# One unit of w_down operands made in the first down phase, and one less beside the gate/up phase of pass 1

## Chip, cores and metric

One core of a Trainium2 chip. The metric is the device time of one execution in microseconds (us), median of several runs. The kernel before: 2275.49 us (2274.35 to 2276.27, 3 runs).

## The reference

```python
x: (8, 1024, 1024)   w_gate, w_up: (1024, 4096)   w_down: (4096, 1024)   # float32
gate = x @ w_gate
up = x @ w_up
gate = 0.5 * gate * (1 + np.tanh(np.sqrt(2 / np.pi) * (gate + 0.044715 * gate ** 3)))
h = gate * up
return (h @ w_down).astype(np.float32)
```

## The kernel before

The 8192 tokens go through in eight passes of 1024. Each pass has a gate/up stage and a down stage. Both use fast (Strassen-like) matrix products in 16-bit floats: passes 0 to 2 with one level of splitting (7 products instead of 8), later passes with a scheme that needs 24 products. Its operands are sums of blocks of the weights, which are made once, in passes 1 to 3, beside the matmuls that run anyway, and kept in DRAM. For w_down this work is cut into eight **units**; one unit is 19 sums on VectorE, six signed copies on ScalarE, and 24 stores of 128 KB (`wd_quads`). Its steps are handed out one by one at set places of the instruction streams.

```python
def wd_unit(u, raw, free):               # raw: where its inputs are loaded; free: output buffers
    nb, j = divmod(2 * u, 8)
    blk = raw.rearrange("p (k c j h) -> p k c j h", k=2, c=2, j=2)
    ...
    def load():
        for k, c, v in ((0, 0, 0), (1, 0, 1), (1, 1, 5)):
            nc.sync.dma_start(out=blk[:, k, c], in_=wdop[2 * v + nb][:, j : j + 2, :])
        nc.gpsimd.dma_start(out=blk[:, 0, 1], in_=wd_eo[0][:, 2 * u : 2 * u + 2, HH:])
    ...
    def step(i):
        stores()                         # of what the step before made, from SyncE
        n, op, a, b = WD_SUMS[i]
        v = at[n] = free.popleft()
        combine(node(n), op, node(a), node(b))               # VectorE
        ...                              # every third step also a signed copy on ScalarE
    return load, [lambda i=i: step(i) for i in range(len(WD_SUMS))] + [stores]

UNITS_ONE = {1: ((0, 4, 4), (1, 108, 4)), 2: ((3, 20, 6),)}   # gate/up: (unit, load at, spacing)
UNITS_DOWN = {1: (2,), 2: (4, 5)}                             # down
UNITS_UP = {3: (6, 7)}
```

In gate/up of passes 1 and 2 there are 16 column tiles of 14 products each, so 224 places; a unit is loaded at the named place and its steps begin 20 places later. GpSimd issues the raw loads of w_gate and w_up for the tiles to come (1 MB each, cast from 32 to 16 bits) at the thirteenth product of each odd tile.

A down stage of these passes is seven products in two halves each, so 14 half-products of 4 x 8 matmuls with 512 columns. In the first one (pass 0), half of w_down (`wd_half`) lies on chip; `half_sum` makes further operands of it in place, `half_store` writes them out, and SyncE issues four DMA transposes for the next pass at the fifth half-product:

```python
half_work = {                            # (half-product, group)
    ...
    (3, 1): [lambda: half_sum(3, 0)], (3, 3): [lambda: half_sum(3, 1)],
    (5, 1): [lambda: half_sum(4, 0)], (5, 3): [lambda: half_sum(4, 1)],
    ...
}
if nb == 0 and g == 0 and p + 1 < NPASS:
    ...
    if v == (2 if p < FAST - 1 else 0):
        transpose_x(p + 1)               # SyncE, 4 transposes
```

## Time and profile before

Stage lengths, from the starts of TensorE's groups in its timeline. Read the second column against the third: where the same matmuls take longer, TensorE waits.

| stage | us | the same matmuls at 215.8 ns each | units made in it |
|---|---|---|---|
| down, pass 0 | 96.69 | 96.7 | 0 |
| gate/up, pass 1 | 205.17 | 193.4 | 2 |
| down, pass 1 | 96.69 | 96.7 | 1 |
| gate/up, pass 2 | 195.58 | 193.4 | 1 |
| down, pass 2 | 96.69 | 96.7 | 2 |

### The profile page before, as it was taken

Reading aid. Unit: us, or ns where it says so; the run is one execution under the profiler, and the core shown is the slowest. Engines: PE = TensorE matmul, PEld = TensorE weight load, DVE = VectorE, ACT = ScalarE, POOL = GpSimd, SP = SyncE. Lnnn points to the kernel's source line nnn. Section 1 sums busy time; section 2 is a strip of 40 time slices with the busy share of each in tenths; the row PEclk is TensorE's granted clock in tenths of the full one; section 3 lists DMA queues with packets and bytes.
Section 4 is the critical chain, followed back from the end, with each engine's and each line's share of the span. In section 5 each row is a group of like instructions: output and inputs, shape, how many; then the busy total and the mean of one; then the engine's idle time right before and its main releaser. Section 6 shows DMA issues by size and latency. Waiting matters only on the chain.

```text
span 2272.0 us, 42804 instructions
## 1 busy us (share of the span) xinstructions
PE 2251.1 (99%) x16639; PEld 1625.5 (72%) x16639; DVE 1560.5 (69%) x2188; ACT 956.3 (42%) x1868; POOL 693.0 (31%) x826
## 2 busy tenths in 40 slices
PE   8999999999999999999999999999999999999999
PEld 4444444444444444888888888888888888888888
DVE  5576368785488864777776677766776667866674
ACT  4443136552155531666115551256403653055520
POOL 1343013430033310455105450145402543034520
PEclk9999999999999999999999999999999999999999
DMA  9998969999999999999998989989999889998876
GB/s 231 176 210 203 263 165 242 247 261 300 254 243 234 244 322 341 336 333 382 309 333 281 312 312 304 333 269 325 298 321 323 278 315 311 323 317 275 282 290 227
DMA packets 308796, 643.50 MB, mean 283 GB/s; under 512 B 79152, under 2 KB 185648, under 8 KB 288048
## 3 DMA queue, kind: packets, MB, share of 16 engines
q1 hardware_dynamic: 253536, 567.36, 73.3%
q0 software_dynamic: 55056, 73.41, 19.4%
q8 instruction: 130, 2.13, 0.4%
q14 instruction: 74, 0.61, 0.1%
HBM read 575.67 MB, written 138.41 MB: 314 GB/s over the span
## 4 chain that ended last, share of the span: by engine, by line
PE 90%; DVE 5%; DMA 3%; issue 1%; ACT 1%; SPq 0%; POOL 0%; DVEq 0%; POOLq 0%; ACTq 0%
PE ps L843 40%; PE ps L1091 20%; PE ps L621 16%; PE ps L983 13%; DMA ring<-in_w_up_dram 2%; DVE ring L350 2%; DVE tmp L640 1%; DVE h_s L278 1%; DMA wd_quads<-x_sums 1%; PE ps L1190 1%; DVE h_a L658 1%; DVE x_sums L278 1%; DMA h_a<-in_x_dram 0%; DMA w_ops<-h_s 0%; ACT ps L637 0%
## 5 line engine op out<-in xcount | busy, mean ns | idle before, releaser
L843 PEld LDWEIGHTS <-ring 128*128 128x128 f16 x8320 | 814.1, 98 | 94.4
L820 POOL TENSOR_TENSOR h_a<-tmp 128x256 f16<-128x256 f32 x640 | 468.3, 750 | 840.3 <-ACT tmp L808 832.7
L843 PE MATMUL ps<-x_sums,ring 128*128 128x256 f16 x5760 | 655.8, 273 | 0.0
L805 DVE TENSOR_TENSOR tmp<-tmp,ps 128x512 f32<-128x512 f32 x640 | 414.4, 683 | 149.3 <-PE ps L843 94.4
L621 PEld LDWEIGHTS <-ring 128*128 128x128 f16 x2632 | 257.5, 98 | 326.6 <-issue 18.4
L790 ACT COPY tmp<-ps 128x512 f32<-128x512 f32 x520 | 303.8, 584 | 237.7 <-PE ps L843 164.8
L621 PE MATMUL ps<-x_sums,ring 128*128 128x512 f16 x1504 | 345.0, 380 | 10.9 <-DVE tmp L640 7.0
L808 ACT ACTIVATE tmp<-tmp 128x256 f32<-128x256 f32 x640 | 263.8, 418 | 173.1 <-DVE tmp L803 79.5
L843 PE MATMUL ps<-x_b,ring 128*128 128x256 f16 x2560 | 305.6, 273 | 0.0
L647 POOL TENSOR_TENSOR h_a<-tmp 128x512 f16<-128x512 f32 x94 | 158.5, 1686 | 362.8 <-ACT tmp L645 223.9
L803 DVE TENSOR_TENSOR tmp<-ps,tmp 128x512 f32<-128x512 f32 x240 | 165.4, 689 | 145.5 <-ACT tmp L790 99.7
L621 PE MATMUL ps<-x_b,ring 128*128 128x512 f16 x1128 | 259.3, 379 | 0.1
L1091 PEld LDWEIGHTS <-h_a 128*128 128x128 f16 x2240 | 219.1, 98 | 25.4
L983 PE MATMUL ps<-ring,h_a 128*128 128x512 f16 x1024 | 222.3, 379 | 0.0
L1091 PE MATMUL ps<-ring,h_a 128*128 128x256 f16 x1920 | 216.1, 273 | 0.0
L983 PEld LDWEIGHTS <-h_a 128*128 128x128 f16 x1152 | 112.7, 98 | 135.9
L640 DVE TENSOR_TENSOR tmp<-ps,tmp 128x512 f32<-128x512 f32 x188 | 127.7, 684 | 114.2 <-ACT tmp L632 111.4
L1148 ACT ACTIVATE tmp<-ps 128x512 f32<-128x512 f32 x60 | 35.4, 597 | 362.5 <-PE ps L1091 274.4
L1160 DVE SCALAR_TENSOR_TENSOR tmp<-ps,tmp 128x512 f32<-128x512 f32 x120 | 81.1, 690 | 97.5 <-PE ps L1091 66.7
L632 ACT COPY tmp<-ps 128x512 f32<-128x512 f32 x188 | 109.8, 584 | 85.9 <-PE ps L621 82.5
L350 DVE TENSOR_TENSOR ring<-ring 128x1024 f16<-128x1024 f16 x188 | 134.2, 726 | 13.8 <-DMA ring<-in_w_up_dram 9.6
L1091 PE MATMUL ps<-ring,x_sums 128*128 128x256 f16 x1120 | 126.4, 273 | 0.0
(94 smaller groups left out, 1535.1 us busy)
## 6 DMA issues: line engine op xcount, KB each, us to landing
ring<-w_ops SPq DMA_DIRECT2D x480, 512.0 KB, 5.0
ring<-wd_quads SPq DMA_DIRECT2D x110, 1024.0 KB, 7.1
ring<-wd_ops SPq DMA_DIRECT2D x35, 1024.0 KB, 7.5
out_dram<-tmp SPq DMA_DIRECT2D x128, 256.0 KB, 6.3
w_ops<-h_s SPq DMA_DIRECT2D x128, 256.0 KB, 6.9
ring<-in_w_gate_dram POOLq DMA_DIRECT2D x23, 1024.0 KB, 11.1
ring<-in_w_up_dram POOLq DMA_DIRECT2D x23, 1024.0 KB, 17.9
wd_quads<-x_sums SPq DMA_DIRECT2D x136, 128.0 KB, 6.2
```

The costliest lines, as they stand in the source:

```text
L350: nc.vector.tensor_tensor(o, a, b, op)
L621: nc.tensor.matmul(ps(b, w), lhs[:, k], rhs[:, k, :], start=(first and k == 0), stop=(k == KH - 1), skip_group_check=True,)
L640: nc.vector.tensor_tensor(o, ps("b", w), o, ADD)
L647: nc.gpsimd.tensor_tensor(hq[TO[n]][:, i, :], tmp[:, t[n, 1]], tmp[:, t[n, 0]], MUL)
L790: nc.scalar.copy(tmp[:, t[o[1]]], ps_all[:, bank[o[2]]])
L803: nc.vector.tensor_tensor(d, b, a, SUB)
L805: nc.vector.tensor_tensor(d, a, b, ADD if o[4] == "add" else SUB)
L808: nc.scalar.activation(d, d, GELU, scale=GSC)
L820: nc.gpsimd.tensor_tensor(h, tmp[:, t[o[1]], MQ : 2 * MQ], g, MUL)
L843: nc.tensor.matmul(ps_all[:, bank[c], w * MQ : (w + 1) * MQ], lhs[:, w, k], rhs[:, k], start=(first and w == 0 and k == 0), stop=(k == KH ...
L983: nc.tensor.matmul(ps_all[:, bank[b, g]], lhs[:, j, g * P : (g + 1) * P], dc[:, n, :], start=(first and j == 0), stop=(j == NP - 1), skip_ ...
L1091: nc.tensor.matmul(ps_all[:, bank[c], m * MQ : (m + 1) * MQ], lhs[:, j, m * P : (m + 1) * P], rhs[:, j, :], start=(first and j == 0 and m ...
```

## The change

Intent: take one unit away from the only stage where TensorE waits much, and make another one in the first down stage, where half of w_down is on chip and VectorE has time. The in-place half-sums of that stage must then come later, as they overwrite what the unit reads.

```diff
     def wd_unit(u, raw, free):
-        blk = raw.rearrange("p (k c j h) -> p k c j h", k=2, c=2, j=2)
+        if raw is not None:
+            blk = raw.rearrange("p (k c j h) -> p k c j h", k=2, c=2, j=2)
...
+                if raw is None:
+                    return wd_half[k][:, j : j + 2, c * MQ : (c + 1) * MQ]
...
-    UNITS_ONE = {1: ((0, 4, 4), (1, 108, 4)), 2: ((3, 20, 6),)}
+    UNITS_ONE = {1: ((0, 60, 6),), 2: ((2, 20, 6),)}
...
-    UNITS_DOWN = {1: (2,), 2: (4, 5)}
+    UNITS_DOWN = {0: (4,), 1: (1,), 2: (3, 5)}
...
-            (3, 1): [lambda: half_sum(3, 0)],
-            (3, 3): [lambda: half_sum(3, 1)],
...
-            (5, 1): [lambda: half_sum(4, 0)],
-            (5, 3): [lambda: half_sum(4, 1)],
-            (6, 0): [lambda: half_store(4)],
-            (7, 0): [lambda: half_store(6)],
+            (6, 2): [lambda: half_sum(3, 0)],
+            (7, 0): [lambda: half_sum(3, 1)],
+            (7, 2): [lambda: half_store(4)],
+            (8, 0): [lambda: half_sum(4, 0)],
+            (8, 2): [lambda: half_sum(4, 1)],
+            (9, 0): [lambda: half_store(6)],
...
-            free = deque(xc[:, j * 512 : (j + 1) * 512] for j in range(24, 38))
+            free = deque(xc[:, j * 512 : (j + 1) * 512] for j in range(24 if p else 32, 38))
+            free.append(spare)
             for i, u in enumerate(UNITS_DOWN[p]):
-                load, fs = wd_unit(u, xc[:, i * 8192 : i * 8192 + 4096], free)
-                steps.setdefault(0, []).append(load)
+                load, fs = wd_unit(u, xc[:, i * 8192 : i * 8192 + 4096] if p else None, free)
+                if p:
+                    steps.setdefault(0, []).append(load)
```

## The prediction

> **What bounds the kernel now.** I read the page first (busy shares, slices), then the table of stretches cut at the stage borders, then TensorE's timeline for every idle gap, then the chain of waits just ahead of the largest gap, and last the DMA issues and VectorE's timeline of the stretch that receives the moved work.
>
> ```profile
> span 2272.0 us, 42804 instructions
> PE 2251.1 (99%) x16639; PEld 1625.5 (72%) x16639; DVE 1560.5 (69%) x2188; ACT 956.3 (42%) x1868; POOL 693.0 (31%) x826
> ```
>
> TensorE is idle for 2272.0 - 2251.1 = 21 us in all, and busy TensorE is at its pace: in the first down phase 96 matmuls of 512 columns start at 228.23 us and the next group at 248.95, so 20.72 / 96 = 215.8 ns each. Whatever this change wins must come out of those 21 us and out of matmuls slowed by a lower clock. Where they are, the stretches tell (first down phase, gate/up of pass 1, down of pass 1, gate/up of pass 2; columns: length, busy us and count of TensorE, its weight loads, VectorE, ScalarE, GpSimd, then granted clock, DMA share, GB/s):
>
> ```profile
> 214.42:311.11 96.69, 96.69 (x449) 43.83 (x448) 46.92 (x51) 11.86 (x20) 5.67 (x5) 1.00 0.89 235
> 311.11:516.28 205.17, 197.09 (x897) 87.83 (x896) 161.83 (x260) 117.46 (x196) 71.40 (x45) 0.99 0.94 243
> 516.28:612.98 96.70, 96.70 (x450) 43.83 (x448) 45.00 (x62) 14.76 (x26) 5.96 (x6) 1.00 0.99 273
> 612.98:808.56 195.58, 194.44 (x898) 87.58 (x896) 156.70 (x241) 114.45 (x190) 65.19 (x46) 1.00 1.00 252
> ```
>
> Gate/up of passes 1 and 2 has the same 896 matmuls, at 215.8 ns at best 193.4 us. Pass 2 takes 195.58, pass 1 takes 205.17. Both make as many entries of the later passes' w_gate/w_up operands; the difference is that pass 1 also makes two units of w_down operands and pass 2 one. Both down phases are without a gap (448 x 215.8 ns = 96.7 us). TensorE's timeline gives the gaps (start, length, group, idle before it):
>
> ```profile
> 390.12 4.65 PE L621 MATMUL ps<-x_sums,ring 128*128 128x512 f16 x20 [1.28 <-DVE tmp L640]
> 442.18 6.06 PE L621 MATMUL ps<-x_sums,ring 128*128 128x512 f16 x20 [2.78 <-DVE tmp L640]
> 494.70 4.48 PE L621 MATMUL ps<-x_sums,ring 128*128 128x512 f16 x20 [1.09 <-DVE tmp L640]
> 664.52 4.48 PE L621 MATMUL ps<-x_sums,ring 128*128 128x512 f16 x20 [0.20 <-DVE tmp L640]
> ```
>
> Pass 1 has ten such gaps from 338 to 495 us, 7.9 us together; pass 2 three, 0.9 us. The worst also leaves a slow group: 6.06 us for 20 matmuls that take 4.48 elsewhere. The chain of waits before it:
>
> ```profile
> 413.67 0.88 POOL ring L335
> 414.55 22.91 DMA ring<-in_w_up_dram
> ...
> 438.16 0.42 DVE spare L278
> ```
>
> The raw w_up load was issued at 413.67, just after the second unit's four loads (410.62 to 412.21), and landed only after 22.91 us. VectorE was then late with the weight sums, the unit's own operation on "spare" stood in line among them, and PSUM was emptied late.
>
> **What the Trainium skill says.** "TensorE: Matmul & The Clock Gate", section "Wait — 56ns, not 53.3ns?", gives 215.7 ns from start to start at 512 columns when warm; the trace's 215.8 agrees, so nothing is to be had from busy TensorE. The same page, section "Part 1: The HAM clock gate", says that an idle window of about 3.4 us brings the half clock back; here the granted clock fell to 0.72 in 442 to 448 us after a gap of only 2.78 us, so the measurement decides: a gap of this size costs 1.58 us on top of itself. "VectorE: DVE Perf Modes", section "The perf-mode tier table", gives 1224 ns for a 16-bit tensor_tensor of 2048 elements; the trace has 1.22. "DMA: Bandwidth & Descriptors", section "Queues, rings and completion order", says that all transfers issued from SyncE share one row of rings and are taken in ring order; the trace agrees, SyncE's stores landing in order of issue, and this is what my main doubt rests on.
>
> **The change, part by part.** There are eight units before and after. Unit 4 moves to the first down phase, and the others shift: pass 1 gate/up makes unit 0 alone (one step every 6 products from product 80, as pass 2 does from product 40) instead of 0 and 1; pass 1 down still makes one unit, pass 2 gate/up one, pass 2 down two. No matmul is added or removed.
>
> *Removed from pass 1 gate/up:* 19 VectorE sums at 0.36 us from start to start (VectorE's timeline in pass 1 down: six from 544.37 to 546.51), 6.8 us of VectorE, six ScalarE copies at 0.62 (3.8 us), 24 stores of 128 KB and four loads of 256 KB. VectorE would be 162 - 6.8 = 155 us busy there, as in pass 2 (156.70). The products at which steps fall modulo 14 are the same set as in pass 2. So I take pass 2 as the measured model: 205.17 - 195.58 = **9.6 us saved**, from 8.5 to 10.3 because the phase of the steps against the pairs differs.
>
> *Added to the first down phase:* the same 19 sums and six copies, without loads, as both halves lie on chip. VectorE has 96.7 - 46.9 = 50 us idle, ScalarE 85 us: by busy time it is free. But there are only seven buffers (six of 512 columns and the spare one) instead of fourteen in pass 1, and a step comes every 5/6 of a slot of eight matmuls (1.73 us), that is every 1.44 us. A buffer is free when its store has landed, and SyncE's order has the four transposes in the middle:
>
> ```profile
> 243.25 0.49 SPq L454 DMA_DIRECT2D wd_ops<-x_sums  x1
> 243.80 19.58 SPq L255 DMA_TRANSPOSE x_b<-x_half  x4
> 263.43 0.60 SPq L454 DMA_DIRECT2D wd_ops<-ring  x1
> 264.13 1.53 SPq L454 DMA_DIRECT2D wd_ops<-x_sums  x1
> 265.76 1.39 SPq L530 DMA_DIRECT2D ring<-wd_ops  x1
> ```
>
> I followed the buffers by hand through the code. Steps 0 to 12 run from 232 to about 249 us. Step 13 takes the buffer of the copy made in step 9, whose store is issued behind the transposes. I put the end of the transposes at 263.4 + 3.4 = 266.8 us (estimate: six 128 KB stores at 0.33 us each and one 1 MB store at about 3.7 us, moved later, go ahead of them, less the 2 to 3 us that the DMA engines idled about 235 us). The store is issued at 267.4 and, as after the transposes of pass 1 (2.5 us from issue to landing), lands at 269.9. So VectorE stands for some 20 us, does steps 13 to 17 by 272, step 18 after one more landing at 273, then the two half_sum of 1.14 us by 275.5. TensorE reads them in its tenth half-product, which starts at 214.42 + 9 x 6.907 = 276.58: **1 us to spare**. The next 1 MB load for the eleventh, issued at 265.76 and landed at 277.2 now, comes behind the last unit store, at about 274, with one 1 MB store and some 0.7 MB of small stores queued before it: landing at 282.5 to 283.5 against a need at 283.49. **No slack.** ScalarE's copy of step 15, which waits for the same landings, also holds the PSUM copies of P6 until about 272, needed at 273.1.
>
> *Sum:* 2275.5 - 9.6 + expected stall. I give no stall 60%, about 1.5 us 25%, about 4 us 15%: 1.0 us. That makes 2266.9 us.
>
> **Rivals.** *A: the saving is whole and the down phase swallows the unit.* For it: 50 us of idle VectorE, and that half_sum was moved back on purpose. Time 2275.5 - 9.6 = 2265.9, or 2264.5 if pass 1 loses still less than pass 2. *B: a wait takes the place of the removed one:* seven buffers behind the transposes stop VectorE and SyncE, and TensorE waits in the tenth and eleventh half-product. For it: the two margins of 1 and 0 us; against it: only a transpose end past 268 us makes over 2 us of it. Time 2268 to 2272. *C: pass 1 keeps its gaps,* because the entries and not the second unit cause them. Against it: pass 2 has as many entries with 0.9 us, and pass 1 has no gap before the first unit's steps begin. Time 2271 to 2275.
>
> **Range and chances.** The ceiling of a gain is pass 1's 205.17 - 193.4 = 11.8 us, 0.5%; over 2% is out of reach. The best case is 2275.5 - 11.8 = 2263.7; a stall of 4 us with 8.5 saved gives 2271.0. I take 2263.5 to 2271.5. A loss of 2% would need 45 us of stall, and nothing that I found can hold TensorE so long.
>
> **What would show it.** Right: gate/up of pass 1 at 195 to 197 us with gaps under 2 us in total and no slow group; VectorE's idle time on x_sums for the landing of wd_quads stores rising by some 20 us in the first down phase; transposes issued until 266 to 268; that phase 96.7 us, or up to 4 us longer with gaps at its tenth or eleventh half-product. Wrong: gate/up of pass 1 still above 199, the first down phase above 101 us, or a new gap in pass 2 or later, where I expect no difference.

## The result

The changed kernel took **2267.85 us** (median of 4 runs, 2267.33 to 2269.77) against 2274.92 us of the kernel before in the same rounds (4 runs). The ratio is 0.9972, 95% interval 0.9954 to 0.9989. Ratios here are the mean time of one kernel's fast runs over that of the other's of the same rounds, so not quite the ratio of the medians quoted. All runs that ratios are taken from are fast (none is over 1.5% above the fastest of its kernel). Where the interval of a ratio leaves out 1, the small difference is clear of the runs' noise. The kernel before had medians of 2272.8 to 2273.5 us beside the experiments.

The page of the changed kernel, to be held against the two lines shown of before:

```profile
span 2265.6 us, 42805 instructions
PE 2249.9 (99%) x16639; PEld 1625.8 (72%) x16639; DVE 1560.5 (69%) x2188; ACT 956.5 (42%) x1868; POOL 687.4 (30%) x825
```

TensorE's idle time fell from 21 to 15.7 us. The table of stretches, cut at the same four stage borders:

```profile
213.82:312.46 98.64, 97.03 (x450) 43.76 (x448) 54.10 (x70) 14.89 (x26) 5.67 (x5) 1.00 0.97 262
312.46:510.42 197.96, 194.76 (x897) 87.62 (x896) 155.82 (x241) 114.56 (x190) 64.38 (x44) 1.00 0.89 232
510.42:607.12 96.70, 96.70 (x450) 43.83 (x449) 45.08 (x62) 14.75 (x26) 5.96 (x6) 1.00 1.00 271
607.12:802.42 195.30, 194.28 (x898) 87.56 (x897) 154.56 (x241) 114.62 (x190) 66.46 (x46) 1.00 1.00 254
```

Gate/up of pass 1 became 7.21 us shorter, the first down stage 1.95 us longer. VectorE's busy time moved as the sums demand: 7.2 us more in the first row, 6.0 less in the second. The rest of the 6.4 us between the two spans lies where the change touches nothing: 0.6 before the first gate/up stage, 0.3 in gate/up of pass 2, 0.3 in the last stage. The first of these varied from 30.0 to 31.0 us over all the profiles, so nothing is built on it.

TensorE's timeline of the changed kernel. Two gaps are new, in the first down stage, and of the ten in pass 1's gate/up four are left:

```profile
273.89 3.61 PE L989 MATMUL ps<-ring,h_s 128*128 128x512 f16 x16 [1.20 <-ACT tmp L914]
284.82 20.89 PE L989 MATMUL ps<-ring,h_a 128*128 128x512 f16 x96 [0.41 <-DMA ring<-wd_ops]
...
389.83 4.48 PE L625 MATMUL ps<-x_sums,ring 128*128 128x512 f16 x20 [2.08 <-DVE tmp L644]
427.16 4.48 PE L625 MATMUL ps<-x_sums,ring 128*128 128x512 f16 x20 [0.53 <-ACT ps L641]
```

**The first down stage.** SyncE's timeline, the row of the four transposes and the load for the eleventh half-product (L534):

```profile
249.11 0.32 SPq L454 DMA_DIRECT2D wd_ops<-x_sums  x1
249.74 18.59 SPq L255 DMA_TRANSPOSE x_b<-x_half  x4
268.43 1.01 SPq L486 DMA_DIRECT2D wd_quads<-x_sums  x2
...
278.28 0.39 SPq L534 DMA_DIRECT2D ring<-wd_ops  x1
```

VectorE's, at step 13 of the unit:

```profile
271.90 0.43 DVE L278 TENSOR_TENSOR x_sums<-x_sums 128x512 f16<-128x512 f16 x1 [19.92 <-DMA wd_quads<-x_sums]
```

ScalarE's, at the copy of step 15 (L505) and the two snapshots of P6 (L914) that stand behind it:

```profile
272.72 0.63 ACT L505 ACTIVATE x_sums<-ring 128x512 f16<-128x512 f16 x1 [19.45 <-DMA wd_quads<-x_sums]
273.26 1.07 ACT L914 ACTIVATE tmp<-ps 128x512 f32<-128x512 f32 x2
```

The stores of steps 9 to 12 stood behind the transposes until 268.4 us; both engines waited almost 20 us for buffers; and the snapshots (the copies of product P6 out of PSUM, the memory in which TensorE sums up) came 1.2 us after TensorE wanted their banks. Why SyncE reached the transposes so late: in all fourteen traces no SyncE transfer is issued before the one eight issues earlier has landed, so it never has more than eight under way. Its last five issues from 245.13 to 249.74 us each begin within 0.06 us of such a landing (245.07 to 249.72). Whether the chip or the program sets the limit is not shown.

The wait that sets the stage's length is the last one. Without any wait the eleventh half-product would begin 10 x 6.907 us into the stage, at 282.89 us; its load, issued behind the unit's stores at 278.28, landed at 284.77, 1.88 us late. The 1.20 us before it only hides most of this.

**Gate/up of pass 1.** The chain of waits before the gap of 2.08 us:

```profile
365.29 20.49 DMA x_sums<-in_w_down_dram
385.77 0.02 issue
385.80 0.43 DVE x_sums L278
```

This is the unit's own load, which GpSimd issued just behind two raw loads (362.25 and 363.18 us). It landed only after 20.49 us, and the unit's first sum, already in VectorE's line, held up everything behind it for 1.79 us. In the kernel before it was the other way round: there the raw load came late behind the unit's.

### The profile page after: what moved, and what is told of

It reads as the page before. It is cut to its first block, busy times and chain, and to the rows that moved or that the text cites. A ratio compares the mean times of both kernels' runs of the same rounds, so it can differ in the third digit from the quotient of the medians.

```text
span 2265.6 us, 42805 instructions
## 1 busy us (share of the span) xinstructions
PE 2249.9 (99%) x16639; PEld 1625.8 (72%) x16639; DVE 1560.5 (69%) x2188; ACT 956.5 (42%) x1868; POOL 687.4 (30%) x825
## 4 chain that ended last, share of the span: by engine, by line
PE 91%; DVE 5%; DMA 2%; SPq 1%; issue 1%; ACT 0%; POOL 0%; DVEq 0%; ACTq 0%
PE ps L847 40%; PE ps L1097 20%; PE ps L625 19%; PE ps L989 11%; DVE ring L350 2%; DVE tmp L644 1%; DMA x_sums<-in_w_down_dram 1%; SPq L255 1%; DVE h_s L278 1%; DMA wd_quads<-x_sums 1%; PE ps L1196 1%; DVE h_a L662 1%; DVE x_sums L278 0%; DMA h_a<-in_x_dram 0%; DMA ring<-wd_ops 0%
## 5 line engine op out<-in xcount | busy, mean ns | idle before, releaser
L651 POOL TENSOR_TENSOR h_a<-tmp 128x512 f16<-128x512 f32 x94 | 153.4, 1632 | 375.1 <-ACT tmp L649 254.4
```

Source lines behind the costliest of these rows:

```text
L651: nc.gpsimd.tensor_tensor(hq[TO[n]][:, i, :], tmp[:, t[n, 1]], tmp[:, t[n, 0]], MUL)
```

## The experiments

The theory: the gain is what one unit less is worth in pass 1's gate/up, less a wait in the first down stage that comes from seven buffers whose stores stand behind the transposes. Its rivals: the place of loads, not the number of units, costs pass 1; a unit costs the same wherever it is put; the down stage's wait has another cause. Diffs are against the changed kernel unless the text says otherwise.

### Transposes later

```diff
-                        if v == (2 if p < FAST - 1 else 0):
+                        if v == ((3 if p == 0 else 2) if p < FAST - 1 else 0):
```

> The changed kernel with the four transposes of the first down phase issued at the seventh half-product instead of the fifth, so that the unit's stores no longer stand behind them. My theory (the phase's 1.95 us over its 96.69 come from SyncE's order: stores behind transposes, seven buffers): VectorE's 19.9 us wait at step 13 shrinks to under 6 us, ScalarE's snapshots come on time, the first down phase takes 96.7 to 97.0 us, the rest stays, so about 1.9 us less than the changed kernel (some 2266 us). Rival (the buffers alone are too few, or the DMA engines are simply full there): the phase stays above 98 us.

Measured: 2266.64 us (5 runs), ratio to before 0.997 (0.9957 to 0.9982). The first down stage took 97.74 us. The gap at the ninth half-product was gone, VectorE's longest wait in the unit was 6.11 us (under 6 expected), but another gap had grown:

```profile
284.78 20.89 PE L989 MATMUL ps<-ring,h_a 128*128 128x512 f16 x96 [0.87 <-DMA ring<-wd_ops]
```

That is the eleventh half-product's 1 MB load, now itself behind the transposes: issued at 275.56, landed at 284.73 us. So the order on SyncE is the cause, and half of the cost was put back by the same cause in another place (the last experiment removes this half too); the expected 96.7 to 97.0 was missed by 0.7.

### The unit's load ahead of the raw loads

```diff
-    UNITS_ONE = {1: ((0, 60, 6),), 2: ((2, 20, 6),)}
+    UNITS_ONE = {1: ((0, 46, 6),), 2: ((2, 20, 6),)}
```

> The changed kernel with unit 0 in gate/up of pass 1 begun at product 46 instead of 60 (same place modulo 14, one column tile earlier), so that its GpSimd load is issued ahead of the raw gate/up loads of the fourth tile and not behind them. My theory (the 2.08 us gap at 389.83 comes from that load landing 20.5 us after issue, which VectorE meets 20 products later): the load lands in under 9 us, no gap above 0.6 us in that stage, pass 1's gate/up takes 195.5 to 196.3 us instead of 197.96, about 2 us less in all. Rival (pass 1 has less room on VectorE than pass 2 whatever the load does): it stays at 197.5 or more, with the gap one tile earlier.

Measured: 2265.37 us, ratio 0.9963 (0.995 to 0.9977). The load landed in 8.1 us. Gate/up of pass 1 took 195.73 us, with three gaps left, of which the largest is

```profile
377.29 4.48 PE L625 MATMUL ps<-x_sums,ring 128*128 128x512 f16 x20 [0.67 <-ACT ps L641]
```

So pass 1 with one unit is as good as pass 2, and the 2.08 us were the load's place. The largest gap left was 0.67 us and not under 0.6.

### Both

> Both edits, the late transposes and the early load. If the two costs are independent: 1.9 + 2.0 us less than the changed kernel, some 2264 us, 0.5% under the kernel before; first down phase 96.7 to 97.0, gate/up of pass 1 195.5 to 196.3. If one hides the other: no better than the better of the two alone.

Measured: 2263.36 us, ratio 0.9955 (0.9943 to 0.9968). First down stage 96.69 us, without a gap, gate/up of pass 1 195.62 us. The load for the eleventh half-product landed at 283.69 us this time, 0.1 us before its need at 283.82. The two savings add up, as they should if the costs are independent.

### The addition alone

```diff
-    UNITS_ONE = {1: ((0, 60, 6),), 2: ((2, 20, 6),)}
+    UNITS_ONE = {1: ((0, 4, 4), (1, 108, 4)), 2: ((3, 20, 6),)}
-    UNITS_DOWN = {0: (4,), 1: (1,), 2: (3, 5)}
+    UNITS_DOWN = {0: (4,), 1: (2,), 2: (4, 5)}
```

> The kernel before with the added part alone: unit 4 is made in the first down phase as in the change, and once more where the kernel before makes it; pass 1's gate/up keeps its two units. My theory: first down phase 98 to 99 us as in the changed kernel, gate/up of pass 1 still 205 us, so 2 us slower than the kernel before (ratio 1.001). Rival (part of the gain comes from the moved half-sums and stores of the first down phase and not from the unit removed): gate/up of pass 1 shorter than 204 us.

Measured: 2273.88 us against 2273.53, ratio 1.0004 (0.9992 to 1.0017). The first down stage took 99.32 us, 2.63 more than before and a little over what was expected. But gate/up of pass 1 took 203.73 us, the rival's side of the line, and pass 2's 195.04, which is why the time hardly moved. Two profiles of the kernel before have 205.17 and 204.99. By the line drawn beforehand for the second of them (205.2 again within 0.3 us, below) the addition did shorten pass 1, by some 1.3 us, and five runs that are no slower in spite of 2.63 us more in one stage agree. But this rests on one profile of the stage (the changed kernel's same stage differed by 1.25 us between two), and its cause was not looked for. The next run has the change's gate/up of pass 1 without the added unit, and there the stage is as short as in the change: its 7.2 us don't need the addition.

### The removal, with the unit put into the down stage of pass 1

```diff
-    UNITS_DOWN = {0: (4,), 1: (1,), 2: (3, 5)}
+    UNITS_DOWN = {1: (1, 4), 2: (3, 5)}
```

> The removal without the addition: as the changed kernel, but unit 4 is made as a second unit of pass 1's down phase and not in the first down phase (correct result). My theory: first down phase 96.7 us, gate/up of pass 1 198 us as in the change, down phase of pass 1 96.7 us as pass 2's with two units, so about 1.9 us less than the changed kernel, some 2266 us. Rival (a unit costs wherever it is put, some 2 us a piece): the down phase of pass 1 takes 98 us or more and the time is that of the changed kernel.

Measured: 2273.66 us against 2273.52, ratio 1.0 (0.9987 to 1.0014): the whole gain was gone in the runs. The profiled one was the fastest of them (2270.19 us, mean granted clock 1.000; the other four 2272.58 to 2274.29 us at 0.998 to 0.999), so the profile shows less than the whole loss. The first down stage was back at 96.69 us and gate/up of pass 1 took 197.97 us as in the change, but the down stage of pass 1 took 101.14:

```profile
579.50 1.89 PE L989 MATMUL ps<-ring,h_a 128*128 128x512 f16 x8 [1.95 <-DVE tmp L918]
583.56 26.06 PE L989 MATMUL ps<-ring,h_a 128*128 128x512 f16 x120 [2.17 <-DVE tmp L918]
```

The first half of the theory holds: without the added unit the first down stage has no wait. The expectation for the second place was wrong. VectorE there waited 13.81 us for a store behind that stage's transposes and, with two units on fifteen buffers, four times more for landings; ScalarE's snapshots stood behind the unit's copies, VectorE's additions behind them. I had taken pass 2's down stage, which makes two units without a gap, as the model, and overlooked that its transposes are issued in the first half-product, ahead of all unit stores, while those of pass 1 come in the fifth, as in pass 0.

### The kernel before with unit 1 begun earlier

Against the kernel before; the unit's loads and steps move together by 10 of the 224 places:

```diff
-    UNITS_ONE = {1: ((0, 4, 4), (1, 108, 4)), 2: ((3, 20, 6),)}
+    UNITS_ONE = {1: ((0, 4, 4), (1, 98, 4)), 2: ((3, 20, 6),)}
```

> The kernel before with unit 1 of pass 1's gate/up begun at product 98 instead of 108, its loads some 10 us ahead of the raw loads instead of just before them; still two units in that stage. Rival to the change (what costs pass 1 is where the unit's loads fall among the raw loads, not that there are two units): the raw load lands in 19 us instead of 22.9, the 2.78 us gap at 442 us and the slow group after it (1.58 us) go, pass 1's gate/up falls to 201 us or less. My theory: that one gap goes or shrinks, but the other gaps (some 5 us) stay, because two units load VectorE more thickly; 200.5 to 203 us, 2 to 4.5 us less than the kernel before and still slower than the change with its own load mended.

Measured: 2269.95 us against 2273.52, ratio 0.9985 (0.9973 to 0.9998). Gate/up of pass 1 took 201.58 us. No gap above 1.3 us was left in it; where 2.78 us and the slow group had been, there are

```profile
440.20 4.48 PE L621 MATMUL ps<-x_sums,ring 128*128 128x512 f16 x20 [0.73 <-ACT ps L637]
453.31 4.65 PE L621 MATMUL ps<-x_sums,ring 128*128 128x512 f16 x20 [0.86 <-ACT ps L637]
```

The raw load landed in 21.5 us, not in the expected 19, but that sufficed. So 3.6 of the 9.4 us by which pass 1 exceeded the mended one-unit stage (205.17 against 195.73) went when the second unit's loads were moved, and 5.85 us (201.58 - 195.73) are left for two units at spacing four against one at six. The edit moved the unit's steps too, so that the 3.6 us are the loads' alone is argued from the gap that went and not shown. The rival has a good third of the truth.

### One unit, but as thickly as before

```diff
-    UNITS_ONE = {1: ((0, 60, 6),), 2: ((2, 20, 6),)}
+    UNITS_ONE = {1: ((0, 46, 4),), 2: ((2, 20, 6),)}
```

> The changed kernel with unit 0 loaded at product 46 and its steps every 4 products instead of every 6. It tells whether the smaller gaps of the kernel before (0.2 to 1.3 us, at 338 to 403 us and 469 to 495 us) come from how thickly the steps stand rather than from the number of units. If thickness: gaps of 0.3 to 1.3 us return in the 76 products of the unit, gate/up of pass 1 198 to 200 us. If not: as with the early load alone, 195.5 to 196.3 us.

Measured: 2267.28 us, ratio 0.9972 (0.9958 to 0.9985); gate/up of pass 1 198.31 us, with gaps such as

```profile
402.21 4.48 PE L625 MATMUL ps<-x_sums,ring 128*128 128x512 f16 x20 [0.86 <-ACT ps L641]
427.42 4.65 PE L625 MATMUL ps<-x_sums,ring 128*128 128x512 f16 x20 [0.85 <-ACT ps L641]
```

That is 2.58 us more than the same unit at spacing six. Twice this, 5.2 us, would be most of the 5.85 us left by the run before it, if the costs of two units add, which no run tests. A unit hurts by how thickly its steps stand, and two units, which share the place for their inputs, fit into 224 places only thickly.

### The unit's copies on VectorE

```diff
+                if raw is None:
+                    nc.vector.tensor_scalar(
+                        v.rearrange("p (j h) -> p j h", j=2), node(m), float(sign), None, MUL
+                    )
+                else:
                     nc.scalar.activation(...)
```

> The changed kernel with the unit's six copies in the first down phase made by VectorE instead of ScalarE, so that ScalarE's snapshots of P6 no longer stand behind a copy that waits for a store. It tells whether the phase's 1.95 us is that one hold or whether three margins lie one behind the other. My theory (all three hang on the transposes' end): the gap at the ninth half-product goes, but gaps at the tenth (half-sums done about 277 us against a need at 276) and the eleventh (load landing about 285 against 283) take its place, and the phase stays at 98.3 to 99.0 us. Rival (the hold alone): the phase falls to 97.2 us or less.

Measured: 2269.22 us against 2272.81, ratio 0.9983 (0.9966 to 0.9999). The first down stage took 100.08 us. The gap at the ninth half-product is gone and those at the tenth and eleventh have taken its place, each with the releaser expected:

```profile
277.36 7.34 PE L994 MATMUL ps<-x_sums,h_s 128*128 128x512 f16 x32 [1.17 <-DVE x_sums L451]
286.32 20.89 PE L994 MATMUL ps<-ring,h_a 128*128 128x512 f16 x96 [1.62 <-DMA ring<-wd_ops]
```

So clearing one wait alone wins nothing: others stand behind it. How much each is worth this run doesn't say. The stage came out 1.1 us above the range expected: with the copies in VectorE's line, step 13 ran at 273.41 us, 1.5 us later than in the changed kernel (0.9 later than in its second profile), and most of the gap at the tenth half-product is that delay: in the changed kernel the first half-sum was done at 275.80, 0.2 us before TensorE would have wanted it at 275.98.

The load explains the stage in every profile. Against 10 x 6.907 us from the stage's start it landed 1.88 us late in the changed kernel, 2.48 in its second profile (below), 0.98 with the transposes later and 3.33 here; the stages are 1.95, 2.55, 1.05 and 3.39 us above 96.69. Profiles with the changed kernel's own order in this stage spread from 98.64 to 99.32 us (five of them).

The profiled run was the slowest of the four (2271.82 us, the others 2268.52 to 2269.69). Its gate/up of pass 1, unmended as in the changed kernel, took 200.69 us, with the gap of the late unit load and a slow group behind it:

```profile
391.70 6.16 PE L630 MATMUL ps<-x_sums,ring 128*128 128x512 f16 x20 [1.98 <-DVE tmp L649]
```

### Before and after once more, and the mended versions beside them

The kernel before, unaltered, profiled again:

> The kernel before, unaltered, for one more profile: how far the stages move from one profiled run to the next. It answers a question of the run with the added part alone, where gate/up of pass 1 took 203.73 us and not 205.17. If the stage spreads by 1.5 us on its own, this profile shows something other than 205.2; if it is 205.2 again within 0.3 us, the added part did shorten pass 1's gate/up.

One run, 2273.96 us, of unknown state for that reason; its profile has gate/up of pass 1 at 204.99 and the first down stage at 96.69 us. The changed kernel, unaltered:

> The changed kernel, unaltered, timed in the same rounds as the two mended ones and profiled once more. First down phase 98.4 to 99.2 us, gate/up of pass 1 197.7 to 198.2 us, ratio to the kernel before 0.997.

Measured: 2269.43 us (2267.86 to 2271.26, 5 runs) against 2273.39, ratio 0.9982 (0.9969 to 0.9994), a smaller gain than at first. First down stage 99.24 us; gate/up of pass 1 199.21 us, 1.0 above what was expected, with one gap that the first profile lacks:

```profile
466.15 4.48 PE L625 MATMUL ps<-x_sums,ring 128*128 128x512 f16 x20 [1.82 <-DVE tmp L644]
```

The chain before it leads to a raw w_up load that took 21.77 us to land. The changed kernel sits at the edge here: five profiles with its pass 1 unmended have 197.96 to 200.69 us, four with the early load at spacing six 195.62 to 196.01. Both edits again, in the same rounds:

> Late transposes and early load once more, in the same rounds as the changed kernel, for a direct ratio: about 4 us (0.2%) less than the changed kernel. In the earlier profile of the late transposes alone the load for the eleventh half-product landed 0.87 us late, behind the transposes; in the one with both edits just in time. Theory (that margin is about zero): the first down phase takes 96.7 to 97.8 us, with any gap at the eleventh half-product.

Measured: 2263.62 us, ratio to before 0.9955 (0.9941 to 0.9968); first down stage 96.69, gate/up of pass 1 196.01 us. Against the changed kernel of the same rounds the means differ by 6.0 us (0.26%), more than the expected 4, in part since the changed kernel was slower than at first (1.1 us in the means). And with the transposes at the ninth half-product, behind the load that they had delayed (diff against both edits):

```diff
-                        if v == ((3 if p == 0 else 2) if p < FAST - 1 else 0):
+                        if v == ((4 if p == 0 else 2) if p < FAST - 1 else 0):
```

> As both edits, but the transposes are issued at the ninth half-product, behind the load for the eleventh. Theory: that load now lands by 276 us, no gap in the first down phase (96.7 us), gate/up of pass 1 195.5 to 196.2 us, time as both edits or up to 1 us less. Rival (the transposes now come too late for the scaling of x and the start of pass 1): a gap at the start of pass 1, gate/up of pass 1 197 us or more.

Measured: **2263.24 us**, ratio to before 0.9955 (0.9942 to 0.9967), 6.2 us (0.27%) under the changed kernel in the means of the same rounds. SyncE's timeline shows the load (L534) ahead of the transposes, and the table of stretches shows the first down stage and gate/up of pass 1:

```profile
264.69 0.40 SPq L534 DMA_DIRECT2D ring<-wd_ops  x1
266.98 0.52 SPq L454 DMA_DIRECT2D wd_ops<-x_sums  x1
267.55 12.92 SPq L255 DMA_TRANSPOSE x_b<-x_half  x4
```

```profile
214.09:310.78 96.69, 96.69 (x449) 43.84 (x448) 54.18 (x70) 14.89 (x26) 5.67 (x5) 1.00 0.96 267
310.78:506.52 195.74, 194.34 (x897) 87.55 (x896) 155.73 (x241) 114.70 (x190) 63.09 (x44) 1.00 0.89 234
```

The transposes were not too late for pass 1. In time this version and the one with both edits are the same; it is the one to keep: here the load landed at 271.15 us, 12 us before its need at 283.16, against 0.1 and 0.9 us in the two profiles of both edits.

| stage, us | before, two profiles | changed, two profiles | both edits (second) | transposes at the ninth |
|---|---|---|---|---|
| down, pass 0 | 96.69, 96.69 | 98.64, 99.24 | 96.69 | 96.69 |
| gate/up, pass 1 | 205.17, 204.99 | 197.96, 199.21 | 196.01 | 195.74 |
| gate/up, pass 2 | 195.58, 195.85 | 195.30, 195.56 | 195.56 | 195.31 |
| whole span | 2272.0, 2272.2 | 2265.6, 2267.7 | 2262.2 | 2261.7 |

## Why the prediction was right or wrong

- **The time**, 2266.9 predicted, 2267.85 and later 2269.43 measured: inside the range both times. Both terms of the sum were off in the same direction, so the gain was smaller than forecast (7.1 us in the medians of the first rounds, 4.0 in the later ones, against 8.6). That the time still fell inside owes something to a range 8 us wide: the saving lay outside its own range, and the stall was twice its mean.
- **The 9.6 us of pass 1's gate/up** came out as 7.2. The model, pass 2, was right for a unit whose load comes ahead of the raw loads: with that mended the stage saves 9.4 us. The term was mis-sized because I checked the phase of the unit's steps modulo 14 and not where its load falls among GpSimd's. The step had its range, 8.5 to 10.3, and 7.2 is outside; so is 5.8 of the second profiles, whose 199.21 us even passes the mark of 199 named as a sign of being wrong. A small slip in the reading of the chain: the w_up load was issued at 414.55, and the 0.88 us at 413.67 are the issue of the w_gate load ahead of it.
- **Rival C**, that the entries (the operands of w_gate and w_up for later passes) and not the second unit cause the gaps, is out: 195.7 us with as many entries and one unit. What the second unit did was two things, which I had not told apart: its loads' place (about 3.6 us) and the thickness of the steps (up to 5.85 us; twice what one unit shows is 5.2).
- **The stall in the first down stage**, expected at 1.0 us as a mean over three cases, was 1.95 us. Rival B's mechanism is what happened, down to the step, though TensorE waited in the ninth and eleventh half-product and not in the tenth and eleventh: VectorE stood at step 13 for 19.92 us ("some 20"). The transposes were issued until 268.3 us, above the estimate of 266.8 and the stated 266 to 268 (2.1 us above, counted from the stage's start), because they began at 249.74 instead of about 244: twelve of the unit's stores, and not the six of the estimate, go ahead of them, and SyncE had to wait for landings with eight transfers under way. I had named three margins, half-sums 1 us, load none, snapshots about 1 us, and called the first two the danger; the third was the first to break, with 1.20 us, and by delaying TensorE it covered all but 0.41 us of the load. The load, 1.88 us late, set the sum: it was named rightly, and came late by about as much as the transposes did. The half-sums were just on time.
- **"By busy time it is free"**: VectorE had 50 us idle there and the unit still cost 2 us. That warning was right, and the fix was not engine time but order on SyncE.
- **The slow group** after the 2.78 us gap went with the gap, as expected. But its reason, the size of the gap, doesn't hold: 1.98 us brought one in the run with copies on VectorE, 2.08 us none in the changed kernel (see the closing list).

## What to carry to other kernels

A stage with idle engines can still have no room: count the buffers, and look at what the queue that frees them has to issue in between; a long issue in the middle of it, here four transposes, sets the time for everybody who waits for a buffer. When work is moved, move its loads and stores by the order of their queue too, not only by the engine's free time: both costs of this change went away by shifting two issues, at no work at all. And where several margins hang on one event, mend the event; taking away the wait that shows only uncovers the next. Ask which wait ends last, and measure it against a schedule without waits.

## What the Trainium skill lacked or had wrong

- "TensorE: Matmul & The Clock Gate", section "Part 1: The HAM clock gate", gives an idle window of about 3.4 us for the half clock and calls the window free-running, but not how idle it has to be. Four traces here have a slow group, after gaps of 1.98, 2.67, 2.77 and 2.78 us (20 matmuls in 6.16, 5.99, 6.06 and 6.06 us instead of 4.48), each with the half clock granted for 3.41 us; after gaps of 2.00, 2.08 and 2.17 us there was none, so the gap's length alone doesn't decide. The clock records agree with a free-running window: full clock lasted 385.71, 436.91, 436.91 and 440.32 us before these, 113, 128, 128 and 129 times 3.4133. Cut into such windows, TensorE was busy for about 42, 24, 31 and 24% of the one just before each half clock. Over all fourteen traces the half clock followed every window of up to 42% and none of 46% or more. This is inferred from the traces, and no run was made to test it.
- "DMA: Bandwidth & Descriptors", section "Queues, rings and completion order", has the ring order (and says that completion need not follow the order of issue; in all fourteen traces SyncE's transfers landed in that order), but not how long SyncE itself stands at issuing: 18.59 us for four transposes in the changed kernel, the first alone 8.52, against a median of 2.54 us over the 28 of that trace (the first of each four took 5.4 to 9.2 us; what holds it isn't shown). Nor does it speak of a limit of eight transfers under way from SyncE, which all fourteen traces keep.
- No page that I read says what the order of one engine's own loads costs: GpSimd's 256 KB cast load took 20.49 us behind two 1 MB cast loads, and 6.8 to 8.1 us ahead of them in the five profiles with the early load.
